# One DMA transpose for a pair of q/k blocks in place of one per block, in a hybrid windowed and dilated attention kernel

## The chip, the core and the metric

The kernel runs on one core of a Trainium2 chip. The metric is device time in microseconds (us) of one execution. A core has five instruction streams that matter here: TensorE (PE, matrix products; its weight loads are shown apart as PEld), VectorE (DVE), ScalarE (ACT), GpSimd (POOL) and SyncE (SP), which here issues nearly all DMAs. Sixteen DMA engines move the data. Each stream runs in its own order, and they meet at semaphores.

## What is computed

The reference is one encoder block on x of 2048 tokens by 1024 features, cut here to what the change touches:

```python
h = rms_norm(x, norm_gain[layer])
proj = h @ w_in[layer]
qa, ka, va, qb, kb, vb, ga, gb, mg = jnp.split(proj, split_idx, axis=-1)
qa = head_rms_norm(qa...) * scale ; ka = head_rms_norm(ka...)
ya, _ = banded_attention(qa, ka, va, A_WINDOW, 1, ...)        # 8 q heads, 2 kv heads, half window 128
for g, (window, dilation) in enumerate(B_GROUPS):             # (128,1), (512,4), (2048,16)
    o, l = dilated_group(qb[:, :, g], kb[:, :, g], vb[:, :, g], window, dilation, ...)   # half window 64
```

Head width is 64. The three B groups are merged by a softmax over their log denominators; both branches are gated, projected to 1024 features, merged and projected once more, and x is added.

## The kernel before, in words

The projections and the attention run in one long stage of 14 **units** (`unit_order`, line 46). A unit is either two kv heads' worth of branch A (kind A: 4 q heads, 1 k head, 1 v head) or two heads of one dilation group of branch B (2 q, 2 k, 2 v heads). For B the group g is 0, 1 or 2, with dilation 1, 4 or 16; a residue class then has n = 16, 4 or 1 blocks of 128 tokens. The units run in the order A, B g1, A, B g2, B g0, and then g1, g2, g0 for each of the other three head pairs.

Each unit takes its 16 blocks as eight **pairs** (class `Pair`, line 678). For a pair PE makes the projection of its two blocks into PSUM (line 695). Both blocks are evacuated, their heads are normed, and each fp32 value is split into an fp16 high and low half (`hi`, `lo`, `swap`; lines 764 to 777) in one tile `spl` of 128 tokens by 2 blocks by 768 values. `swap` makes two POOL copies, the first for the first block and the second for the second. Then `turn` (line 779) issues a DMA transpose for each block on SP: 128 x 768 fp16 values of `spl` become six 128 x 128 tiles in a tile called `kq`. First blocks of a residue class (where the unit has more than one block to the class) go to a tile `kq0` with three buffers, because the last item of the class needs them once more; the rest go to `kq` with six buffers.

An **item** (class `Item`, line 789) is the attention of two heads for one query block. `logits` (line 830) makes the scores on PE from `kq` (line 845): the query block is the weight, the key blocks are the moving side. A B item of g0 or g1 reads its own block and the next one, a g2 item its own alone, an A item the one before, its own and the next. So of the items that a pair makes possible, the first needs only the first block of the pair, and the following one the second. The probabilities are split as well and turned by a DMA transpose of their own into `pt` (line 883; 1536 columns for an A item inside the sequence, 1024 for g0 and g1, 512 for g2), and PE multiplies them with v (line 894).

The order of every engine's stream is written out by hand: `at(t, f)` puts a step at a time on a list, the unit of time being one pair of projections (about 9 to 14 us), and `until` issues what is due between the projection matmuls. `Pair.plan` (line 700) puts the nine steps of the norm behind the end of the pair's projection by the offsets `NORM` (line 62): `swap` at 1.155 and `turn` at 1.24 pairs. `Item.plan` puts `logits` 2.899 pairs behind the pair's start (`LS`, line 63), two items of a B pair half a pair apart. PE takes the scores in that order, between projection matmuls; when a `kq` block has not landed, PE stands. SP holds, in the same kind of order, the transposes of `kq` and `pt`, the stores and loads of partial results (`zd`, `zz`, `ytd`, `gtd`) and the weight loads (`wraw`). A DMA is told complete by one semaphore count, so a reader of `kq` waits for the whole transpose that wrote it.

Behind this stage come the other projections and the branch, merge and output products, which the change does not touch.

## Time and profile before

| | us |
|---|---|
| median of 3 timed runs | 1924.89 |
| lowest and highest of them | 1921.34 and 1925.0 |
| the profiled execution, its own time | 1920.61 |
| its span, first to last instruction | 1918.8 |
| PE busy in the span | 1872.6 |
| first and last `kq` transpose issued at | 97.2 and 1204.8 |

The profiled execution is one execution, 4.3 us shorter than the median of the timed runs; 1.8 us of its time lie outside the span. The granted TensorE clock was 0.999. In views of the trace, "SPq" is an instruction of SP's queue; its duration is the time that the queue took to issue the DMA, and "landing" is the time from the start of that issue to the completion count.

### The profile page before, as it was taken

The page shows a single profiled execution, that of the slowest core. Times are in us where ns is not written, and L with a number is a line of the kernel's source. Part 1 is how long each engine was busy: PE and PEld are TensorE (multiplying, and loading weights), DVE is VectorE, ACT ScalarE, POOL GpSimd, SP SyncE. Part 2 cuts the span into 40 slices and gives each one's busy share as a digit, 9 for nine tenths or more (in the row PEclk, how much of TensorE's full clock was granted, in tenths as well). Part 3 has the DMA queues.
Part 4 walks back from the last instruction along what each step waited for, and adds up shares of the span by engine and source line. Part 5 has one row for each costly group of instructions (what it writes and reads, how often), then busy time and mean ns, then how long its engine had stood idle before and what let it go on. Part 6 is the DMA issues. An engine that isn't in the chain of part 4 may idle for free.

```text
span 1918.8 us, 51078 instructions
## 1 busy us (share of the span) xinstructions
PE 1872.6 (98%) x19242; PEld 1438.2 (75%) x19242; DVE 1502.6 (78%) x3835; ACT 1250.0 (65%) x3015; POOL 578.4 (30%) x1363
## 2 busy tenths in 40 slices
PE   6999999999999999999999999999999999999998
PEld 4567987789999899998999898544444446776774
DVE  7689778986887889878789888657778754987885
ACT  8477768886776777777767766565675875433441
POOL 1034334353553435543455445200000001222121
PEclk9999999999999999999999999999999999999999
DMA  6259998987888679988897777776565658854551
GB/s 255 83 105 194 163 187 140 191 167 164 168 149 182 136 156 202 151 161 172 147 171 153 146 150 143 172 275 196 177 211 175 190 186 271 273 160 120 148 150 64
DMA packets 643448, 326.21 MB, mean 170 GB/s; under 512 B 459265, under 2 KB 598145, under 8 KB 640769
## 3 DMA queue, kind: packets, MB, share of 16 engines
q1 hardware_dynamic: 643056, 322.70, 72.7%
q8 instruction: 150, 2.46, 0.6%
q14 instruction: 98, 0.79, 0.1%
q10 hardware_dynamic: 144, 0.26, 0.0%
HBM read 139.08 MB, written 73.66 MB: 111 GB/s over the span
## 4 chain that ended last, share of the span: by engine, by line
PE 85%; DMA 7%; DVE 3%; ACT 2%; SPq 2%; issue 1%; POOL 0%; DVEq 0%; POOLq 0%; ACTq 0%
PE pj L695 42%; PE fps L1577 17%; PE fps L1961 7%; PE fps L1889 6%; PE s L845 5%; PE pv L894 4%; DMA pt<-p 3%; PE pj L302 2%; DMA kq<-spl 1%; PE pj L350 1%; PE fps L302 1%; DMA xt<-in_x_dram 1%; PE pt L958 1%; SPq L1874 1%; DMA bigl<-sd 1%
## 5 line engine op out<-in xcount | busy, mean ns | idle before, releaser
L695 PE MATMUL pj<-wl,XH 128*128 128x128 f16 (+2 forms) x2816 | 716.2, 268 | 0.0
L695 PE MATMUL pj<-wh,XL 128*128 128x128 f16 (+2 forms) x2816 | 712.5, 269 | 0.0
L695 PE MATMUL pj<-wh,XH 128*128 128x128 f16 (+2 forms) x2816 | 709.7, 268 | 0.0
L695 PEld LDWEIGHTS <-XH 128*128 128x128 f16 x5632 | 575.3, 112 | 54.5
L695 PEld LDWEIGHTS <-XL 128*128 128x128 f16 x2816 | 316.1, 112 | 24.0
L860 DVE CUSTOM_DVE_ANT_0 pr<-s,b,ubuf 128x256 f32<-128x256 f32 (+3 forms) x512 | 218.9, 465 | 43.1 <-PE s L845 40.6
L877 DVE SCALAR_TENSOR_TENSOR p<-pr,p 128x512 f16<-128x512 f32 (+2 forms) x256 | 195.3, 763 | 53.0 <-ACT p L873 50.2
L762 POOL TENSOR_TENSOR rw<-rw,g 128x128 f32<-128x128 f32 (+1 forms) x224 | 149.1, 685 | 204.9 <-DVE rw L755 186.5
L1899 POOL TENSOR_TENSOR g<-g,t 128x512 f32<-128x512 f32 x32 | 48.5, 1515 | 529.6 <-DMA g<-mgd 384.9
L1577 PEld LDWEIGHTS <-wh 128*128 128x128 f16 x1064 | 104.1, 98 | 126.1 <-issue 3.1
L713 ACT ACTIVATE rw<-pj 128x256 f32<-128x256 f32 (+1 forms) x224 | 87.3, 390 | 132.5 <-PE pj L695 131.9
L777 POOL COPY spl<-spl 128x256 f16<-128x256 f16 (+1 forms) x224 | 97.0, 462 | 245.4 <-DVE spl L772 245.4
L873 ACT ACTIVATE p<-pr 128x512 f16<-128x512 f32 (+2 forms) x256 | 157.7, 616 | 16.3 <-DMA pt<-p 11.9
L1889 PE MATMUL fps<-y,bigh 128*128 128x128 f16 x1792 | 153.7, 219 | 2.8 <-DVE r L1822 2.8
L845 PE MATMUL s<-kq 128*128 128x128 f16 (+1 forms) x1856 | 148.3, 218 | 4.4 <-DMA kq<-spl 3.3
L1961 PE MATMUL fps<-WO,mf 128*128 128x512 f16 x672 | 150.3, 379 | 2.4 <-DVE xr L1968 2.4
L1889 PE MATMUL fps<-y,bigl 128*128 128x128 f16 x896 | 151.8, 219 | 0.0
L1889 PEld LDWEIGHTS <-bigh 128*128 128x128 f16 x1792 | 139.1, 98 | 10.5 <-issue 3.1
L845 PEld LDWEIGHTS <-kq 128*128 128x128 f16 x2016 | 130.9, 98 | 20.8 <-issue 5.5
L894 PE MATMUL pv<-vt,pt 128*128 128x65 f16 (+1 forms) x2784 | 132.1, 193 | 9.3 <-DMA pt<-p 9.3
L894 PEld LDWEIGHTS <-pt 128*128 128x128 f16 x3024 | 119.6, 98 | 25.1 <-DMA pt<-p 12.9
L768 ACT ACTIVATE spl<-rw 128x512 f16<-128x512 f32 (+1 forms) x112 | 72.1, 643 | 79.9 <-POOL vt L724 71.1
(250 smaller groups left out, 3812.7 us busy)
## 6 DMA issues: line engine op xcount, KB each, us to landing
wraw<-in_w_units_dram SPq DMA_DIRECT2D x56, 384.0 KB, 4.9
g<-mgd SPq DMA_DIRECT2D x64, 256.0 KB, 4.8
wraw<-in_w_mrg_dram SPq DMA_DIRECT2D x45, 256.0 KB, 5.0
mgd<-t SPq DMA_DIRECT2D x43, 256.0 KB, 3.2
zd<-z SPq DMA_DIRECT2D x128, 66.0 KB, 2.0
zz<-zd SPq DMA_DIRECT2D x64, 132.0 KB, 3.4
xt<-in_x_dram SPq DMA_DIRECT2D x16, 512.0 KB, 7.8
ytd<-yo SPq DMA_DIRECT2D x32, 256.0 KB, 3.5
```

The lines of the kernel that those rows point to most:

```text
L695: out.append(lambda lhs=lhs, rhs=rhs, ch=ch, a=a, b=b, k=k: T.matmul(ps[:, a:b], lhsT=lhs[:, ch, :], rhs=rhs[:, ch, a:b], start=(k == 0), ...
L713: A.activation(self.rw[:, n * i:n * i + n], self.ps[i][:, :n], AF.Copy)
L762: G.tensor_tensor(q[:, i, :un.nq, :], q[:, i, :un.nq, :], g, OP.mult)
L777: G.tensor_copy(sp[:, i, nh:, :, :], sp[:, i, nq:nh, ::-1, :])
L845: T.matmul(self.sv[j][:, o:o + k1 - k0], lhsT=q[:, h, :], rhs=kt[:, un.nq + kh + v * un.nk, k0:k1], start=(v == 0), stop=(v == 1))
L860: V.tensor_tensor_reduce(out=self.pv[:, j, self.p0:self.p0 + W], in0=self.sv[j], in1=un.bias[:, self.h0 + j, self.b0:self.b0 + W], scale=I ...
L873: A.activation(self.sp[:, :128 * n], self.pr, AF.Copy, scale=PSC)
L877: V.scalar_tensor_tensor(self.sp[:, 128 * n:], self.pr, PSC, self.sp[:, :128 * n], OP.mult, OP.subtract)
L894: T.matmul(self.po[:, j, :w], lhsT=p[:, n * j + s, :], rhs=un.v[key][:, vh, c0:c0 + w], start=(k == 0 and s == 0), stop=(k == 2 and s == n ...
L1577: T.matmul(b[k][:], lhsT=w[:, i, ch, :], rhs=xform(PROD[i][0], lo, ch, q), start=(i < 3 and n == 0), stop=(n == 11), skip_group_check=True)
L1889: out.append(lambda p=p, c=c, wl=wl, yl=yl, n=n: T.matmul(ps[:, 128 * p:128 * p + 128], lhsT=w[wl][:, i, c, p, :], rhs=y[:, yl, c, :], sta ...
L1961: out.append(lambda p=p, ml=ml, wl=wl, k=k: T.matmul(ps[:], lhsT=m[:, ml, p, :], rhs=WO[:, i, wl, p, :], start=(fresh and k == 0), stop=(k ...
```

## The change

The two blocks of a pair are turned by one DMA transpose of 1536 columns into one tile of twelve 128 x 128 tiles. The only exception is the first pair of a g0 unit (four pairs of the 112), which keeps two transposes: its first block goes to a tile of its own, `kq0`, now with one buffer, because it is read again at the end of the unit. `kq` has four buffers of double size in place of six, and `kq0` one in place of three: 4 x 12 + 6 = 54 tiles of 128 x 128, as before (6 x 6 + 3 x 6). No other step or due time is altered.

```diff
-KQ_BUFS = 6
+KQ_BUFS = 4
...
         def turn(self):
+            kq = wk.tile([128, 12, 128], F16, name="kq", bufs=KQ_BUFS)
+            if self.un.shift and self.un.n == NT and self.subsets[0][1] == 0:
+                k0 = wk.tile([128, 6, 128], F16, name="kq0", bufs=1)
+                parts = (k0[:], 0, 1), (kq[:, 6:], 1, 2)
+            else:
+                parts = (kq[:], 0, 2),
+            for k, a, b in parts:
+                nc.sync.dma_start_transpose(out=k, in_=self.sp[:, a:b].rearrange("p s a b c -> p (s a b c)"))
             for i, s in enumerate(self.subsets):
-                if self.un.shift and s[1] == 0:
-                    kq = wk.tile([128, 6, 128], F16, name="kq0", bufs=3)
-                else:
-                    kq = wk.tile([128, 6, 128], F16, name="kq", bufs=KQ_BUFS)
-                nc.sync.dma_start_transpose(out=kq[:], in_=self.sp[:, i].rearrange("p a b c -> p (a b c)"))
-                self.un.kq[s] = kq
+                self.un.kq[s] = parts[0][0] if i == 0 and len(parts) == 2 else kq[:, 6 * i:6 * i + 6]
```

## The prediction

> **What bounds the kernel now.** I read the page first: the busy times, and the chain that ended last by engine.

> ```profile
> span 1918.8 us, 51078 instructions
> PE 1872.6 (98%) x19242; PEld 1438.2 (75%) x19242; DVE 1502.6 (78%) x3835; ACT 1250.0 (65%) x3015; POOL 578.4 (30%) x1363
> PE 85%; DMA 7%; DVE 3%; ACT 2%; SPq 2%; issue 1%; POOL 0%; DVEq 0%; POOLq 0%; ACTq 0%
> ```

> PE is busy for 98% of the span. A change to a DMA moves the time only by way of moments at which PE stands, so the second view is the list of PE's waits, cut to the stage with transposes (92 to 1236 us).

> ```profile
> PE pv L894 <- DMA pt<-p: 9.3, 9, 2.8
> PE s L845 <- DMA kq<-spl: 3.3, 3, 2.2
> ```

> The columns are total us, times, longest. PE stood nine times for turned probabilities and three times for turned q and k, 12.6 us together. Even if the change removed every one, it could win no more than that: 0.65% of the span. What it can lose has no such bound, because each landing that comes later than PE needs it stops PE, and PE is the engine that sets the end.

> **What an issue and a landing cost.** The third view is line 785 (the `kq` transposes), whole and in one quiet moment, beside the `pt` transposes of other widths, each in a quiet moment: one of a g2 item (512 columns, 688 us) and one of an A item (1536 columns, 142.3 us).

> ```profile
> L785 SPq DMA_TRANSPOSE kq<-spl x224: 1209/1238/3286, 97.2 to 1204.8; - x112
> DMA to landing us min/median/max: 2.7/3.2/8.1
> ```

> ```profile
> L785 SPq DMA_TRANSPOSE kq<-spl x2: 1222/1232/1243, 132.2 to 133.5; - x2
> DMA to landing us min/median/max: 2.7/2.8/2.8
> ```

> ```profile
> L883 SPq DMA_TRANSPOSE pt<-p x1: 1207/1207/1207, 688.0 to 688.0; - x1
> DMA to landing us min/median/max: 2.4/2.4/2.4
> ```

> ```profile
> L883 SPq DMA_TRANSPOSE pt<-p x1: 1441/1441/1441, 142.3 to 142.3; - x1
> DMA to landing us min/median/max: 3.7/3.7/3.7
> ```

> The issue hardly grows with the width: 1.21 us for 512 columns, 1.23 for 768, 1.44 for 1536. The landing does: 2.4, 2.8 and 3.7 us, about 0.33 us more for each 256 columns. The merged transpose has the shape of the A item's, so both of its prices are in this trace: 1.44 us of SP, 3.7 us to land.

> **The change, part by part.**

> *SP's queue.* 108 of 112 pairs go from two issues to one: 2 x 1.24 - 1.44 = 1.0 us less, 1.1 us with the gap between the two, some 115 us of SP in all. SP is not on the path by itself. This is worth something only where a DMA that PE waits for stands directly behind a `kq` pair.

> *When the blocks are there, in a quiet moment.* Before, counted from the first issue: first block 2.8 us, second 1.3 + 2.8 = 4.1 us. After: both at 3.7 us. The first block comes 0.9 us later, the second 0.4 us earlier.

> *The wait added.* The first transpose so far waits only for its own block's POOL copy; the merged one waits for both. The row below shows both copies, ending at 501.21 + 0.74 = 501.95, while the first transpose (quoted further down) was issued at 501.7.

> ```profile
> 501.21 0.74 POOL L777 COPY spl<-spl 128x256 f16<-128x256 f16 x2 [1.86 <-DVE spl L772]
> ```

> So where POOL is what SP waits for, the issue moves 0.2 to 0.3 us back, and the first block comes up to 0.9 + 0.3 = 1.2 us later. Behind the waiting issue on SP stand a `pt` transpose, stores and loads; as the pair takes 1.1 us less, they still start earlier than before.

> *Buffers.* Four tiles of a pair hold the last four pairs, where six of a block held three. A pair's blocks are last read by items of the next pair's turn (in g1 by the class's last item, also there). So no new wait for a buffer; I cost this at nothing. If it were otherwise SP would wait on PE at line 785.

> *Who pays for the first block's lateness.* I followed the chain of waits through the stage and looked for pieces "DMA kq<-spl": PE went on exactly at such a landing, with no slack at all.

> ```profile
> 501.72 6.17 DMA kq<-spl
> 531.12 6.55 DMA kq<-spl
> 980.33 5.32 DMA kq<-spl
> 1202.60 5.68 DMA kq<-spl
> ```

> All four are the first block of a pair in a g0 unit. There the landing is not quiet: it shares the DMA engines with partial results and weights and takes 5.3 to 6.6 us. What a merged transpose would do there I bound by the landing of the second block, which closes the same 1536 columns. First and last of the four:

> ```profile
> L785 SPq DMA_TRANSPOSE kq<-spl x2: 2255/2283/2311, 501.7 to 504.1; - x2
> DMA to landing us min/median/max: 4.4/5.3/6.2
> ```

> ```profile
> L785 SPq DMA_TRANSPOSE kq<-spl x2: 2006/2054/2101, 1202.6 to 1204.8; - x2
> DMA to landing us min/median/max: 4.1/4.9/5.7
> ```

> The first lands at 501.7 + 6.2 = 507.9, the second at 504.1 + 4.4 = 508.5: 0.6 us. In the last it is 1208.3 and 1208.9: 0.6 us. The four give 0.6 to 0.7 each, 2.4 us. I then set every other first block's landing against the start of the matmul that reads it. Eight more pairs, six of them in g0 units, have less slack than their two landings lie apart. The first, the widest and the last of the eight, each with the scores that read them:

> ```profile
> L785 SPq DMA_TRANSPOSE kq<-spl x2: 1211/1296/1380, 172.1 to 173.4; - x2
> DMA to landing us min/median/max: 4.1/4.4/4.7
> ```

> ```profile
> L845 PE MATMUL s<-kq x8: 218/219/220, 177.2 to 177.6; 128*128 128x128 f16 x8
> ```

> ```profile
> L785 SPq DMA_TRANSPOSE kq<-spl x2: 1234/1892/2550, 726.4 to 729.0; - x2
> DMA to landing us min/median/max: 5.0/5.1/5.2
> ```

> ```profile
> L845 PE MATMUL s<-kq x6: 218/220/220, 732.1 to 732.4; 128*128 128x128 f16 x6
> ```

> ```profile
> L785 SPq DMA_TRANSPOSE kq<-spl x2: 1210/1220/1231, 1193.7 to 1195.0; - x2
> DMA to landing us min/median/max: 3.3/3.5/3.7
> ```

> ```profile
> L845 PE MATMUL s<-kq x8: 219/219/220, 1197.5 to 1197.9; 128*128 128x128 f16 x8
> ```

> At 172.1 they land at 176.8 and 177.5 and the new block is read amid these scores, at 177.4: 0.1 us of new standing. At 726.4 they land at 731.4 and 734.2, read at 732.2: 2.0. At 1193.7 they land at 1197.4 and 1198.3, read at 1197.6: about 0.6. The eight give 0.1 to 2.0 each, 7.7 together. Twelve places, upper end 2.4 + 7.7 = 10.1 us. Lower end: everywhere the merged transpose ends the 0.4 us earlier that it gains in a quiet moment, 10.1 - 12 x 0.4 = 5.3 us. I take **6.5 us**, nearer to the lower end, because four of the eight have landings 1.6 to 3.4 us apart, where the second transpose was held up on its own, which the merged one need not be. Elsewhere the first block has more slack than that, and no second block is late.

> *Who gains from SP.* In the A units the probabilities queue behind the `kq` pair. One such place in SP's order of time, and PE's stands that follow from such `pt` transposes:

> ```profile
> 143.79 2.89 SPq L785 DMA_TRANSPOSE kq<-spl  x2
> 146.84 3.52 SPq L883 DMA_TRANSPOSE pt<-p  x2
> ```

> ```profile
> 152.38 0.71 PE L894 MATMUL pv<-vt,pt 128*128 128x65 f16 x18 [0.72 <-DMA pt<-p]
> 180.93 0.72 PE L894 MATMUL pv<-vt,pt 128*128 128x65 f16 x18 [2.26 <-DMA pt<-p]
> 383.55 0.63 PE L894 MATMUL pv<-vt,pt 128*128 128x65 f16 x15 [0.64 <-DMA pt<-p]
> ```

> Five of PE's nine stands for `pt` (the two others are 0.23 and 0.50 us) hang on a transpose that was issued right behind a `kq` pair or one small load later. With 1.1 us at most for each they could give back 0.7 + 1.1 + 0.2 + 0.5 + 0.6 = 3.1 us. Lower end nothing, where the DMA engines and not SP hold the transpose. In the window 297 to 402 us, an A unit, the DMA engines are almost never idle:

> ```profile
> 297.00:402.00 105.00, 102.72 (x1304) 82.88 (x1303) 95.89 (x247) 92.03 (x215) 42.16 (x88) 1.00 0.96 171
> ```

> The last but one column is their busy share, 0.96. So I take two thirds: **2.0 us**.

> [...]

> **Sum.** +6.5 - 2.0 = +4.5 us. Against the profiled execution's own 1920.6 us that is 1925.1; against the median of the runs shown, 4.3 us above that execution, 1924.9 + 4.5 = **1929 us**, slower by 0.23%. A measurement of this kernel can tell about 0.2%, 3.9 us, from no change; so this forecast stands just beyond that.

> **Rivals.**

> 1. *Faster: SP's queue was the limit of the A units.* Place: units 0 to 2, 97 to 402 us. If the 1.1 us that SP gains in each pair reach every `pt` transpose, all nine stands shrink, not five, and up to the whole 9.3 us goes; it decides from where that gain is over the 6.5 us lost in g0, or these are absorbed as in rival 2. With -7 and +3: 1921 us; the best end is 1924.9 - 9.3 = 1916. For it: SP issues the `pt` back to back there. Against it: the DMA share of 0.96. Chance 0.13.
> 2. *No difference: the losses are not added up.* PE's stand in an early pair of a g0 unit gives POOL and DVE time to catch up, and the later pairs of the unit are less late. Then each of the six units with such places pays its largest item alone: 0.1 + 1.0 + 0.6 + 2.0 + 1.6 + 0.6 = 5.9, less 6 x 0.4, that is 3.5 us, and 2 to 3 come back in the A units: 1924.9 + 1 = 1926 us. For it: PE's list has only three stands at twelve tight places. Against it: the pair behind starts from PE's own progress, so a stand moves its chain too. Chance 0.36.
> 3. *The merged transpose isn't one transfer of this price.* If it went as two, the issue would be 2.5 us and nothing would move: 1925 us. The 1.44 us row for the same shape speaks against it; it is part of the 0.36.

> **Numbers.** Forecast (slower by over 0.2%) 0.51, within 0.2% 0.36, faster 0.13. For the forecast alone the range is 1924.9 + (5.3 - 3.1) to 1924.9 + 10.1, 1927 to 1935. The three runs shown lie 3.7 us apart, so I add 2 us above: 1937. Below I reach through rival 2 and into rival 1: 1920.

> **What would show it.** Right: 116 issues at line 785 with about 1.44 us each; quiet landings of 3.7 us; PE's wait for `kq` up from 3.3 to about 8 to 10 us, with the largest pieces in the g0 units (475 to 548, 700 to 772, 922 to 996, 1146 to 1216 us); PE's wait for `pt` down from 9.3 to about 7. Wrong: PE's wait for `kq` unchanged (the chain has more slack than I read, or moves with PE), landings of the merged transpose far from 3.7 us in quiet moments, a wait of SP on PE at line 785 (buffers), or `pt` waits that vanish.

## The result, and the profile after

The change makes the kernel slower by 0.17%: over 14 executions each, the ratio is 1.0017 with a 95% interval of 1.0009 to 1.0024, a loss of 3.3 us (1.7 to 4.6). The means, 1925.36 us against 1922.08 us before, lie 3.3 us apart; the medians, 1925.74 and 1921.39 us, lie further apart, 4.35 us. The median of before used for the prediction (1924.89) came from the first three of these 14 executions.

The first surprise is the profile. The execution that was profiled took 1920.06 us, the shortest of the 14, and its span is not longer than that of before. The page, the same three lines as in the prediction:

```profile
span 1918.2 us, 50899 instructions
PE 1871.8 (98%) x19242; PEld 1438.4 (75%) x19242; DVE 1503.1 (78%) x3835; ACT 1249.7 (65%) x3015; POOL 580.0 (30%) x1363
PE 83%; DMA 7%; DVE 4%; ACT 2%; issue 2%; POOL 1%; SPq 1%; DVEq 0%; POOLq 0%; ACTq 0%
```

The list of PE's waits in the stage with transposes (line, released by, total us, times, longest) shows two large movements that almost cancel. The lines of `kernel.py` behind `turn` have moved by three: 848 is the scores' line, 897 that of the values.

```profile
PE s L848 <- DMA kq<-spl: 10.0, 10, 1.8
PE pv L897 <- DMA pt<-p: 2.7, 3, 1.8
```

The wait for `kq` rose from 3.3 to 10.0 us, the wait for `pt` fell from 9.3 to 2.7 us. Line 787, the transposes, whole and in one quiet moment:

```profile
L787 SPq DMA_TRANSPOSE kq<-spl x116: 1209/1518/5480, 97.9 to 1201.4; - x116
```

```profile
L787 SPq DMA_TRANSPOSE kq<-spl x1: 1415/1415/1415, 641.8 to 641.8; - x1
DMA to landing us min/median/max: 3.7/3.7/3.7
```

116 issues in place of 224; the one in the quiet moment took 1.42 us of SP's queue and landed after 3.7 us, with a DMA share of 0.66 over these 3.7 us. Where more was under way it is another matter: the chain of waits has nine pieces that end at a `kq` landing, 5.8 to 7.7 us long, with a DMA share of 1.06 to 1.29 over each. The first is in the first g1 unit; the other eight are in g0 units, where before had four and none elsewhere:

```profile
272.62 6.05 DMA kq<-spl
494.42 7.67 DMA kq<-spl
525.44 7.16 DMA kq<-spl
721.43 6.79 DMA kq<-spl
742.02 6.88 DMA kq<-spl
947.25 6.75 DMA kq<-spl
967.81 6.53 DMA kq<-spl
978.57 5.93 DMA kq<-spl
1201.41 5.80 DMA kq<-spl
```

The eight take 5.8 to 7.7 us; the four of before took 5.3 to 6.6. At the first of the eight PE's scores show what such a landing does: two matmuls on the item's own block, which is there, then 1.84 us of nothing, then the rest.

```profile
500.01 0.28 PE L848 MATMUL s<-kq 128*128 128x128 f16 x2
502.13 0.49 PE L848 MATMUL s<-kq 128*128 128x128 f16 x6 [1.84 <-DMA kq<-spl]
```

### The profile page after: what moved, and what is told of

Read it like the earlier page. It is cut to its first block, busy times and chain, and to the rows that moved or that the text cites. A ratio compares the mean times of both kernels' runs of the same rounds, so it can differ in the third digit from the quotient of the medians.

```text
span 1918.2 us, 50899 instructions
## 1 busy us (share of the span) xinstructions
PE 1871.8 (98%) x19242; PEld 1438.4 (75%) x19242; DVE 1503.1 (78%) x3835; ACT 1249.7 (65%) x3015; POOL 580.0 (30%) x1363
## 4 chain that ended last, share of the span: by engine, by line
PE 83%; DMA 7%; DVE 4%; ACT 2%; issue 2%; POOL 1%; SPq 1%; DVEq 0%; POOLq 0%; ACTq 0%
PE pj L695 40%; PE fps L1580 17%; PE fps L1964 7%; PE fps L1892 6%; PE s L848 5%; PE pv L897 4%; DMA kq<-spl 3%; DMA pt<-p 2%; PE pj L350 2%; PE pj L302 1%; PE fps L302 1%; PE pt L961 1%; DMA bigl<-sd 1%; DVE pr L863 0%; PE s L480 0%
## 5 line engine op out<-in xcount | busy, mean ns | idle before, releaser
L777 POOL COPY spl<-spl 128x256 f16<-128x256 f16 (+1 forms) x224 | 97.4, 464 | 247.5 <-DVE spl L772 247.5
L848 PEld LDWEIGHTS <-kq 128*128 128x128 f16 x2016 | 131.2, 98 | 28.0 <-issue 12.6
```

What stands on the lines that cost most here:

```text
L777: G.tensor_copy(sp[:, i, nh:, :, :], sp[:, i, nq:nh, ::-1, :])
L848: T.matmul(self.sv[j][:, o:o + k1 - k0], lhsT=q[:, h, :], rhs=kt[:, un.nq + kh + v * un.nk, k0:k1], start=(v == 0), stop=(v == 1))
```

## The experiments

My theory: (1) a pair's first block is there later, PE stands for it where it has no slack, above all in g0 units, and this costs; SP's shorter queue lets the `pt` transposes of the A units go earlier, and this gains. The rival: (2) the loss comes from something that the whole kernel carries, the larger tiles and fewer buffers, or from the merged transfer being slow as such.

Every run below was timed against before on its own chip. "kq" and "pt" are PE's waits from 92 to 1236 us in that run's one profile.

| run | merged where | ratio to before, 95% interval | kq, us | pt, us |
|---|---|---|---|---|
| change | all | 1.0017 (1.0009 to 1.0024) | 10.0 | 2.7 |
| e11 | all, the change once more | 1.0012 (1.0000 to 1.0024) | 12.2 | 4.8 |
| before | none | 1 | 3.3 | 9.3 |
| e6 | none, before once more | 1.0002 (0.9992 to 1.0012) | 3.1 | 9.2 |
| e3 | none, the change's tiles | 1.0011 (1.0001 to 1.0021) | 3.1 | 7.8 |
| e2 | g0 alone | 1.0037 (1.0022 to 1.0051) | 8.9 | 7.7 |
| e4 | none, g0's second block first | 1.0036 (1.0022 to 1.0049) | 9.9 | 7.3 |
| e1 | all but g0 | 0.9999 (0.9986 to 1.0011) | 7.6 | 1.6 |
| e5 | A units alone | 0.9990 (0.9981 to 0.9999) | 3.3 | 5.6 |
| e9 | all, g0 scores later | 0.9998 (0.9986 to 1.0010) | 8.1 | 3.7 |
| e10 | A units alone, g0 scores later | 0.9980 (0.9967 to 0.9993) | 0.8 | 6.9 |
| e12 | none, g0 scores later | 0.9995 (0.9986 to 1.0005) | 2.4 | 8.4 |

**Which units pay, which gain: e1, e2.** In `turn`, a condition chooses two transposes into the two halves of the pair's tile; in e2 it is negated, `not (...)`. The lines between are left out:

```diff
+            two = self.un.kind == "B" and self.un.g == 0
...
+            elif two:
+                parts = (kq[:, :6], 0, 1), (kq[:, 6:], 1, 2)
```

> Merged transposes everywhere but in the four g0 units, which go back to one transpose per block (the tiles of the change are kept). Theory 1 (the change costs by the first block's later landing in g0 units and gains by SP's shorter queue in the A units): PE's wait for kq falls back to about 3 us, its wait for pt stays near 3 us, and the time is 3 to 6 us below before, ratio 0.997 to 0.9985. Theory 2 (the loss comes from something that the whole kernel carries, such as the larger tiles and fewer buffers): the ratio stays at about 1.0017.

> The reverse: merged transposes in the g0 units alone (without the first pair of each, as in the change), one per block in all others. Theory 1: wait for kq about 10 us, wait for pt about 9 us as before the change, time 6 to 7 us above before, ratio 1.003 to 1.004. Theory 2: about 1.0017, as the change.

e2 came out as theory 1 has it: 1.0037, and its list of waits shows the `kq` side of the change without the gain on the `pt` side.

```profile
PE s L851 <- DMA kq<-spl: 8.9, 9, 1.5
PE pv L900 <- DMA pt<-p: 7.7, 9, 2.8
```

e1 missed its size: 0.9999, not 0.997 to 0.9985. Its waits say why in part: `pt` is as low as expected, but `kq` stayed at 7.6.

```profile
PE s L851 <- DMA kq<-spl: 7.6, 8, 2.2
PE pv L900 <- DMA pt<-p: 1.6, 3, 0.8
```

Two of those eight stands, 1.72 and 0.85 us, are in the first g1 unit, whose pairs are still merged. So first blocks are tight in a g1 unit too. Five others, 4.85 us, are in the g0 units, whose pairs have single transposes here; in the three profiles of before, e6 and e3 those units have 3.1 to 3.3 us. So this one profile does not show the return to 3 us that theory 1 expects. The losses of e1 and e2 add up to 0.36% where the change has 0.17%; their intervals just allow that.

**Tiles alone, and the order of landing: e3, e4.** e3 uses two transposes in every pair (`two = True`), with the change's tiles and buffers. e4 is e3 with this loop:

```diff
-            for k, a, b in parts:
+            for k, a, b in (parts[::-1] if self.un.kind == "B" and self.un.g == 0 else parts):
```

> The tiles and buffers of the change, but one transpose per block everywhere, so that only tiles and buffers differ from before. Theory 1: no difference, ratio 1.000 within 0.001, wait for kq about 3 us, for pt about 9 us. Theory 2: the loss of the change stays, ratio about 1.0017.

> As the run with the change's tiles and one transpose per block everywhere, but in the g0 units the second block's transpose is issued first. Nothing is merged; only the first block comes later. Theory 1: in a quiet moment the first block lands 4.1 us after the first issue (merged 3.7, before 2.8), so the stands in g0 are as large as with the merged transposes or larger, kq 10 to 14 us in all, pt about 9 us, time 6 to 10 us above before, ratio 1.003 to 1.005. If the merged transfer itself is what is slow (its size, not the order of landing), the ratio is within 0.001 of 1.

e4 shows that a late first block is enough, without a slow merged transfer: nothing is merged, the first block of a g0 pair is only issued second, and the loss is 0.36%, as in e2 (0.37%), with much the same waits.

```profile
PE s L851 <- DMA kq<-spl: 9.9, 8, 2.1
PE pv L900 <- DMA pt<-p: 7.3, 8, 2.3
```

e3 is less clean. Its waits are close to those of before, as theory 1 expects, but its ratio is 1.0011 with an interval that just leaves out 1. The order of every engine's stream in its trace is that of before. So up to 0.2% may hang on the tiles themselves. Its profile says where it lost time: the same PE matmul comes 0.1 us later than in before's at 1300 us, and 2.95 us later at 1700. Between the two, in the output products behind this stage, PE waits longer for `xr`, first in before, then in e3 (from 1236 us on):

```profile
PE fps L1961 <- DVE xr L1968: 2.4, 2, 1.5
PE fps L1967 <- DVE xr L1974: 3.6, 2, 2.8
```

The rest of it is a stretch of 3.4 us right behind the longer stand, in which the granted TensorE clock is half (0.997 over e3's span, 0.999 over before's; see the last section). Eight of the eleven profiles with the change's tiles have this longer stand (over 2 us), the change's first profile not among them, and none of the three with the tiles of before. No run here tells the tiles from chance.

**How much is scatter: e6, e11.** Before, and the change, each once more:

> The kernel before, unchanged, as a measure of what a tenth of a per cent means here: ratio 1.000 within 0.001; PE's wait for pt 8 to 10 us and for kq 2 to 5 us if the first profile was typical. If the run with the change's tiles alone (1.0011) was only scatter, this one scatters by as much.

> The change once more, on the chip of the other two, with a profile of its own. The first profile of the change was the shortest of its 14 runs and its waits (10.0 for kq, 2.7 for pt) nearly balance, while the median is 3.3 us above before. If that profile had a lucky share of landings, this one shows more: kq 10 to 12, pt 3 to 6 us, ratio 1.0015 to 1.002. If the two waits are again 12 to 13 us together and the ratio is again 1.0017, the loss of the median lies outside these waits.

e6 gave 1.0002 and the waits of the first profile within 0.2 us. e11's profile answers the surprise of the section above: in this execution, of 1928 us, both waits are larger.

```profile
PE s L848 <- DMA kq<-spl: 12.2, 10, 2.0
PE pv L897 <- DMA pt<-p: 4.8, 5, 1.9
```

Together 17.0 us, against 12.7 in the change's first profile and 12.6 and 12.3 in the two of before. The two samples of the change give +4.4 and +0.1 us over the first of before, and the measured 3.3 lies between. The second execution was 8.4 us longer than the first, though, and these waits make 4.3 of it. The stand for `xr` behind the stage makes 1.2 more (3.6 us in place of 2.4), and two whole stretches at half clock, behind 753.3 and 1682 us, where the first execution had none (granted clock 0.998 over the span, 1.000 in the first), up to 1.7 us each (an estimate, see the last section).

**The A units alone: e5.** Merged only where the unit is of kind A (`two = self.un.kind == "B"`).

> Merged transposes in the two A units alone, one per block in all B units (the change's tiles). The merged g1 pairs had cost PE 2.6 us of waits in unit 1 in the run with g0 split. If SP's shorter queue in the A units is the gain and late first blocks are the cost wherever they occur, then: wait for kq about 3 us, wait for pt about 2 to 4 us, time 3 to 5 us below the run with one transpose per block everywhere, that is ratio 0.998 to 0.9995 against before. If the gain in the A units was only chance of one execution, pt stays at 7 to 9 us and the ratio is 1.000 to 1.001.

0.9990, kq 3.3, pt 5.6 us. The direction is that of SP's shorter queue; `pt` fell less than I expected, and less than in e1 (1.6). The difference lies mostly in the first A unit, which both merge (4.6 us of stands here, 1.0 us there), so it is the scatter of single executions and not the g1 unit's share.

**Later items: e7, e8.** If PE stands because the scores' place in the order is too early, later items of g0 should mend it. I moved whole items:

```diff
-                nxt = max(nxt, t + LS + (L_LAST if t == NPAIR - 1 else 0))
+                nxt = max(nxt, t + LS + (L_LAST if t == NPAIR - 1 else 0) + (.15 if un.kind == "B" and un.g == 0 else 0))
```

> The change, with the items of the g0 units 0.15 of a pair (about 1.4 us) later in the written order; no transfer is altered. If PE stands there only because the first block lands 0.5 to 1.8 us after the scores' place in the order, the waits for kq fall from 10 to 2 to 4 us and the time is 4 to 7 us below the change, ratio 0.998 to 0.9995 against before. If the lateness moves with PE, or the later items only push the stand elsewhere (values, merges), the sum of PE's waits stays and the ratio stays at 1.001 to 1.002.

> Merged in the A units alone, and the items of the g0 units 0.15 of a pair later: both gains without the cost. Wait for kq under 2 us, wait for pt 2 to 4 us, time 5 to 8 us below before, ratio 0.996 to 0.9975. If later items cost elsewhere, it is no better than the run merged in the A units without them.

Both failed badly: ratios 1.0366 (1.0350 to 1.0382) and 1.0371 (1.0358 to 1.0384), some 70 us. e7's waits, here from 92 to 1320 us, show a new one:

```profile
PE pj L695 <- DVE vt L731: 30.8, 48, 1.4
PE pt L187 <- ACT wl L211: 14.9, 10, 2.1
```

`nxt` never falls back within the B units, so every later item's steps on DVE and ACT moved too, against the pairs' own steps: the evacuation of v (line 731) now stands behind an item's step on DVE, and the projections wait for their PSUM bank. With 3.6 us of the same kind for `vw` these waits are some 49 of the 70 us; the rest is not traced here. The question was not answered by it.

**Only the scores later: e9, e10, e12.** The same idea with one lever: only the score matmuls of g0 move, 0.055 of a pair, in PE's order; all other engines' orders are untouched.

```diff
-                at(s + d, f)
+                at(s + d + (.055 if f == self.logits and un.kind == "B" and un.g == 0 else 0), f)
```

> The change, with only the score matmuls of the g0 items moved in PE's own order, 0.055 of a pair (about 0.5 us of projection matmuls) behind their place; the order of every other engine and of SP is untouched. If the stands are the lateness of the first block against that place, each of the eight or nine g0 stands shrinks by up to 0.5 us: wait for kq about 6 us, time 3 to 4 us below the change, ratio 0.9995 to 1.0005 against before. If the scores are what DVE then waits for, that gain is lost again and the ratio stays at 1.0015 to 1.002.

> Merged in the A units alone, with the same move of the g0 scores: wait for kq about 2 us, for pt 5 to 6 us, time 1 to 2 us below the run merged in the A units alone, ratio 0.998 to 0.9985 against before. If DVE pays for later scores, ratio 0.999 or above.

> The kernel before with nothing but the move of the g0 scores in PE's order, 0.055 of a pair later; no transposes merged. It divides the gain of the run that had both (0.998). If the two parts add up, the move alone takes the kq waits from 3 to about 1 us and leaves pt at 8 to 10 us: 1 to 2.5 us below before, ratio 0.9987 to 0.9995. If the move is all of the gain, the ratio is 0.998 as there; if it is none, 1.000.

e9 took the change from 1.0012 (e11, same chip) to 0.9998, about 3 us as expected; so the loss in g0 is lateness against the scores' place. Its `kq` wait in the one profile, 8.1 us, is above the 6 I expected, but 2.2 of it stand in the first g1 unit, whose scores e9 does not move. In the g0 units it is 5.95 us, against 9.2 and 10.05 in the two profiles of the change. e10 joins the part that gains (A units) with the move, and beats both kernels: 0.9980, 1917.34 us, where the change on that chip took 1925.34 and before 1922.26.

```profile
PE pv L900 <- DMA pt<-p: 6.9, 7, 2.4
PE s L851 <- DMA kq<-spl: 0.8, 1, 0.8
```

e12, the move without any merging, is 0.9995, not told apart from 1; e5, merging without the move, is 0.9990. The two parts add up to e10 within their intervals, though on three chips.

## Why the prediction was right or wrong

**Lateness of the first block, +6.5 us: right, if anything small.** PE's wait for `kq` rose by 6.7 us in the first profile and by 8.9 in the second. The prices were right (1.42 us of SP for 1.44, 3.7 us to land for 3.7), and the place: of the ten stands of the first profile, nine are in g0 units and one in the first g1 unit; e2 and e4 show that the first block's landing alone makes the loss, merged or not. The bound by the old second block's landing held for the sum, though not place by place: at 494.4 PE now stands 1.84 us where I had 0.6.

**Gain from SP's queue, -2.0 us, at most 3.1: the mis-sized term.** It measured 6.6 us in the first profile and 4.5 in the second (9.3 less 2.7 and 4.8): the waits for `pt` did not stop at the 7 us that I had named as the sign of being right. SP shows the gain where the prediction showed the queue:

```profile
144.18 1.81 SPq L787 DMA_TRANSPOSE kq<-spl  x1
146.09 7.75 SPq L886 DMA_TRANSPOSE pt<-p  x3
```

From the start of the `kq` issue to that of the next `pt` it is now 1.9 us, where it was 3.05 (143.79 to 146.84): 1.1 us, as priced. Two of the stands behind such issues are left:

```profile
152.15 0.54 PE L897 MATMUL pv<-vt,pt 128*128 128x65 f16 x12 [0.32 <-DMA pt<-p]
180.26 0.41 PE L897 MATMUL pv<-vt,pt 128*128 128x65 f16 x8 [1.81 <-DMA pt<-p]
```

The five stands that I had named shrank from 4.35 to 2.2 us (these two and one of 0.09, too short for the list of waits), as predicted. What I left at nothing, the four that were not directly behind a `kq` pair, shrank too, from 4.94 to 0.7 us, and to 2.3 in the second profile. The largest of them, 2.75 us up to 200.81 (its line is in the last section), is gone, and with it about 1.5 us at half clock behind it; the same matmuls start at 196.20 now:

```profile
196.20 0.70 PE L897 MATMUL pv<-vt,pt 128*128 128x65 f16 x18
```

SP's queue in those units is a chain of `pt` and `kq` issues, and what was won at one place was carried on to the next. The rows of SP ahead of that place show it, two of before and two of the change:

```profile
187.61 3.14 SPq L785 DMA_TRANSPOSE kq<-spl  x2
193.85 7.77 SPq L883 DMA_TRANSPOSE pt<-p  x3
184.29 1.94 SPq L787 DMA_TRANSPOSE kq<-spl  x1
190.14 7.02 SPq L886 DMA_TRANSPOSE pt<-p  x3
```

SP's lead over before grows from 1.9 us at the pair ahead (170.21 for 172.09) to 3.3 here and 4.5 at the next (197.21 for 201.71), while PE's own lead, at the stand of 188.21, was 1.55 us. I had tied the gain to the neighbour in the queue, and let the DMA share of 0.96 argue against more. Rival 1 described this (all nine shrink); the faster kernel that it gave as the net did not come, because the loss in g0 is as large or larger.

**Sum.** Forecast +4.5 us, measured +3.3 (1.7 to 4.6). That the two are so near is in part luck: both terms came out larger than forecast (6.7 and 8.9 us lost for 6.5, 6.6 and 4.5 won for 2.0), and their errors offset each other. The measured 0.17% lies below the 0.2% that I set as the border, and its interval reaches across it to 0.24%; so by the ratio, of my three cases it was "within 0.2%" that came true, to which I gave less than to "slower". The mechanism that I gave that case, stands of a unit absorbing each other, is not what the traces show: the stands add up, as the forecast had it, and it is the gain in the early units that pays for them: for half in the second profile, for nearly all in the first. The predicted 1929 us lies 3.3 us above 1925.74, about as far as the 1924.89 us of three executions lay above the 1921.39 us of fourteen.

**Buffers at nothing.** SP's list of waits has none on PE at line 787, so this held. But e3 leaves a part of 0.11% (0.01 to 0.21) that its waits in this stage do not explain; in its one profile the loss lies behind the stage. Whether that hangs on the tiles stays open.

**Rival 3** is out: one issue of 1.42 us.

## What to carry to other kernels

Here merging two transfers saved 1.1 us of issue time on the queue, measured at 144.18 us, and took from the first reader the early half: in a quiet moment 3.7 us to land in place of 2.8. Before merging, set each first half's landing against the start of its first reader, stage by stage: here the same edit gained in the units where PE waited for what stood behind it in the queue, and lost in the units where PE read the first half at the moment it landed. Doing it only in the former, and moving the readers in the latter by half a microsecond without merging there, was better than all or nothing. A change of this size can look like none in a single profile; a second profile of the same kernel showed what the first, taken in the shortest execution, had hidden.

## What the runs showed of the hardware

In the trace of before a stand of PE cost more than its own length: PE stood 2.75 us up to 200.81 us, and the granted clock then was half (0.50) for 3.4 us. The rows are three stretches (us, busy times by engine, the granted clock, DMA share, GB/s):

```profile
200.81 1.16 PE L894 MATMUL pv<-vt,pt 128*128 128x65 f16 x18 [2.75 <-DMA pt<-p]
```

```profile
190.00:200.00 10.00, 8.06 (x132) 7.76 (x129) 7.74 (x21) 7.77 (x18) 3.17 (x10) 1.00 1.04 164
200.60:204.00 3.40, 3.19 (x31) 2.64 (x31) 1.97 (x5) 2.84 (x6) 0.00 (x0) 0.50 1.18 236
204.00:214.00 10.00, 10.00 (x164) 9.95 (x163) 8.22 (x23) 7.69 (x21) 3.09 (x5) 1.00 0.99 184
```

A stretch like this can cost up to another 1.7 us, an estimate from its 3.4 us at a clock of 0.50. Here it cost about 1.5, estimated from two leads: the change's matmuls were 4.6 us ahead of the same ones of before at 200.81 (now 196.20), and 6.15 us at 227.16 (now 221.01), with nearly equal stands at the latter (0.57 and 0.55 us). In the second profile of the change the same follows a `kq` stand of 2.03 us at 753.3, with 0.50 from 753.9 to 757.3. The stand of 1.84 us at 502 in the change's first profile had no such stretch behind it (clock 1.00 from 502 to 509), nor had one of 2.60 us at 181 in e6 (clock 1.000 over its whole span).

```profile
197.19:200.60 3.41, 0.87 (x16) 0.71 (x13) 1.70 (x6) 1.11 (x4) 0.85 (x5) 1.00 1.12 129
176.38:179.79 3.41, 2.26 (x27) 1.98 (x25) 3.31 (x8) 1.61 (x3) 2.46 (x4) 1.00 1.23 186
179.79:183.20 3.41, 1.96 (x41) 1.97 (x42) 3.07 (x8) 1.89 (x5) 0.78 (x3) 1.00 1.29 273
```

In before and the change's first profile, from the first record of the clock on (23.1 and 25.1 us) to the span's end, two whole steps had PE idle for more than 1.9 us. Both are in before, the one above with 2.5 us and one at 1914.07 us with 2.3, and behind both the clock was 0.50; the other whole steps of the two traces had 1.87 us or less, and behind each of them the clock was 1.00. In the second profile of the change PE idled 2.03 us (10.80 less 8.77) from 743.00 to 753.80, just ahead of its stretch at 0.50. So it was in these three traces; no run tested it by itself.
